# RG-LRU coefficients from an exponential of the gate, and a 16-token decay product moved to GpSimd, in a two-layer hybrid trunk

## The chip, the cores and the metric

The kernel runs on one core of a Trainium2 chip. The metric is the device time of one execution, in microseconds (us); the time of a kernel is the median of its runs. The engines are named as in the profile: PE is TensorE (matmuls; PEld is its weight load), DVE is VectorE, ACT is ScalarE, POOL is GpSimd, and SP issues the DMAs. A row's line number is a line of the kernel before.

## The reference, cut to what matters

Two layers, each a feed-forward half step, a mixing step with four mixers side by side (A: RG-LRU, B: gated delta rule, C: SSD, D: S5), and a second feed-forward half step, on 272 tokens of width 1024. The change touches mixer A and one product of mixer C:

```python
def rglru_mixer(u_x, u_gate, conv_w, conv_b, w_a, b_a, w_i, b_i, lam, norm_g):
    xc = (causal_dwconv(u_x, conv_w) + conv_b).astype(F32)
    ...
    r = jax.nn.sigmoid(... xh, w_a ... + b_a)
    ig = jax.nn.sigmoid(... xh, w_i ... + b_i)
    log_a = -LRU_C * r * jax.nn.softplus(-lam.astype(F32))     # LRU_C = 8
    a = jnp.exp(log_a)
    b = jnp.sqrt(-jnp.expm1(2.0 * log_a)) * (ig * xc)
    _, h = lax.associative_scan(_linear_combine, (a, b), axis=1)
    y = jax.nn.gelu(u_gate.astype(F32)) * h
    return rms_norm(y, norm_g)
...
    # mixer C, in ssd_chunked: scores of a chunk times their decays
    y_diag = jnp.einsum("bcgls,bcgels,bcsgep->bclgep", cb, lmat, x)
```

## The kernel before, in words

Activations lie feature-major: 128 features on the partitions, 272 tokens (256 in the last layer, after the mixing) on the free axis. All projection weights come from HBM in chunks of 128x1024 (512 KB), three raw buffers deep (`load`). For each chunk `ahead` makes two pieces, `hi` by a copy on ACT (L215) and `lo` by a subtraction on DVE (L217), four buffers deep, and PE multiplies a chunk in 24 matmuls of three kinds (`mm3`, L232 to L234). These chunk matmuls, called g matmuls below after their PSUM tile `g`, are the bulk of PE's time; those of the mixers themselves write PSUM tiles `m`, of which there are four.

The mixing step is a list of steps written out by hand (`STEPS_TEXT`). The list gives each instruction its priority; the scheduler of the tile framework (`schedule_with_timeline_sim=True`) makes from it one fixed order for each engine, putting a step of later priority ahead where its model of the time has an engine free and the earlier step not ready. On the chip each engine goes through its own order strictly, so an instruction that waits holds up all that are behind it on its engine.

In the list the steps that matter here come as `... am2 am1 ... am0 ... am3 bs04 bf12 S0 bf13 ce0 bf14 ag0 bs10 bs11 cz3 bs12 ac ag1 bs13 bs14 bz0 S1 bz1 as0 ...`:

- `am0` to `am3` (`a_gates`): for each of the four 128-feature blocks, two matmuls, three tanh on ACT (L887, L888, L889) and a product on DVE (L890). L888 makes t = tanh(-log_a/2) into the tile `s5a` (`at_`).
- `ac` (`a_coef`): from t it makes a = 2/(1+t) - 1 and sqrt(1-a^2) = 2 sqrt(t)/(1+t). Four square roots on ACT (L897) after a load of ACT's function table; for each block a sum (L901), a reciprocal (L902) and a multiply-add (L903) on DVE and two products on POOL (L904, L905), the last into `s5b` (`ab_`).
- `as0` to `as3` (`a_scan`): the recurrence, on DVE (L915).
- `bs00` to `bs14` (`b_solve`) and `bf00` to `bf14` (`b_factor`): the triangular solve of mixer B, a serial chain between PE (L686) and ACT or DVE. `bf14` copies a factor `f4t` from PSUM on ACT (L707, tile `rk`); `bs10` subtracts the first block's part on DVE (L722, tile `rs`). The PE step `bs11` (L686, `m<-rs,rk`) needs both of them.
- `S0`, `S1` (`decay_in`): 10 small copies on ACT each (L501), the input of the decay matmuls of `ce0` and `ce1`.
- `ce0` to `ce3` (`c_decay`): decay matmuls (L517 to L525), three exponentials on ACT (L528), then the product with the scores: 832 columns on POOL (L815) and the last 16 tokens on DVE (L816). `cp0` to `cp3` (`c_pair`) multiply the result on PE (L826).

Temporary tiles `r` are a ring of nine, given out in the order of the list.

Of the kernel before, what the change touches and what calls it, by code (L numbers as in the profile page):

```python
# [12 lines left out]
AF = mybir.ActivationFunctionType  # L13
ALU = mybir.AluOpType
AX = mybir.AxisListType.X

P = 128
T = 272
# [99 lines left out]
class Trunk:  # L118
# [693 lines left out]
    def c_decay(s, i):  # L812
        e = s.ce[i] = s.decay(s.R[2 + i])
        gt = s.cg[:, i // 2:i // 2 + 1, :]
        s.nc.gpsimd.tensor_tensor(out=e[:, :, 0:416], in0=gt[:, :, 0:416].to_broadcast([P, 2, 416]), in1=e[:, :, 0:416], op=ALU.mult)  # L815
        s.nc.vector.tensor_tensor(out=e[0:16, :, 416:432], in0=gt[0:16, :, 416:432].to_broadcast([16, 2, 16]), in1=e[0:16, :, 416:432], op=ALU.mult)  # L816


    def c_pair(s, i, l):
# [24 lines left out]
    def a_consts(s):  # L844
        nc = s.nc
        c = COLS
        cut = lambda n: s.sm[:, :, c[n][0]:c[n][0] + c[n][1]]

        m = s.tiny([P, 2, 4], 'lm')
        nc.vector.tensor_scalar(out=m, in0=cut('llam'), scalar1=-1.0, scalar2=None, op0=ALU.mult)  # L850
        sp = s.softplus(m, [P, 2, 4])
        s.sp2 = s.const([P, 2, 4], 'sp2')
        nc.vector.tensor_scalar(out=s.sp2, in0=sp, scalar1=2.0, scalar2=None, op0=ALU.mult)
        s.hb = s.const([P, 2, 8], 'hb')
        o = c['lba'][0]
        nc.vector.tensor_scalar(out=s.hb, in0=s.sm[:, :, o:o + 8], scalar1=0.5, scalar2=None, op0=ALU.mult)
# [21 lines left out]
    def a_gates(s, i, l):  # L878
        nc = s.nc
        xc, w = s.ab_[:, i, :], s.lw[i]  # L880
        pr, pi = s.mps(), s.mps()
        nc.tensor.matmul(pr[:, 0:T], lhsT=w[:, 0, :], rhs=xc, start=True, stop=True)
        nc.tensor.matmul(pi[:, 0:T], lhsT=w[:, 1, :], rhs=xc, start=True, stop=True)
        t = s.at_[:, i, :]
        sp = s.sp2[:, l, i:i + 1]
        r, g = s.tmp(), s.tmp()
        nc.scalar.activation(out=r, in_=pr[:, 0:T], func=AF.Tanh, scale=0.5, bias=s.hb[:, l, i:i + 1])  # L887
        nc.scalar.activation(out=t, in_=r, func=AF.Tanh, scale=sp, bias=sp)  # L888
        nc.scalar.activation(out=g, in_=pi[:, 0:T], func=AF.Tanh, scale=0.5, bias=s.hb[:, l, 4 + i:5 + i])  # L889
        nc.vector.scalar_tensor_tensor(out=xc, in0=g, scalar=1.0, in1=xc, op0=ALU.add, op1=ALU.mult)  # L890


    def a_coef(s):
        nc = s.nc
        sq = [s.tmp() for _ in range(4)]
        for i in range(4):
            nc.scalar.activation(out=sq[i], in_=s.at_[:, i, :], func=AF.Sqrt)  # L897
        for i in range(4):
            t, b = s.at_[:, i, :], s.ab_[:, i, :]
            r = s.tmp()  # L900
            nc.vector.tensor_scalar(out=t, in0=t, scalar1=1.0, scalar2=None, op0=ALU.add)  # L901
            nc.vector.reciprocal(out=r, in_=t)  # L902
            nc.vector.tensor_scalar(out=t, in0=r, scalar1=2.0, scalar2=-1.0, op0=ALU.mult, op1=ALU.add)  # L903
            nc.gpsimd.tensor_tensor(out=b, in0=b, in1=sq[i], op=ALU.mult)  # L904
            nc.gpsimd.tensor_tensor(out=b, in0=b, in1=r, op=ALU.mult)  # L905

    def a_gate(s, ps, i):
        if i == 0:
# [404 lines left out]
    def mixing(s, l, sl, done):  # L1313
        s.R, s.be, s.ce, s.bm, s.bo, s.cacc = ({} for _ in range(6))
        s5 = {}
        s.sl, s.N = sl, sl.stop - sl.start

        def small():
            s.sm16 = s.tokens(s.small_tile())

        def d_in(u):
            s5[u] = s.d_load(l, u)
            s.d_in(u, s5[u])

        def rin(i):
            s.R[i] = s.decay_in(i)

        def chain():
            with s.tc.issue_after(s.last_dve):
                s.b_chain()  # L1330

        do = dict(
            sm=small, tk=lambda: s.token_scalars(s.sm16, l), R=rin, S=lambda i: rin(2 + i),
            di=d_in, do=lambda u: s.d_out(u, s5[u]), da=lambda f: s.d_act(f, l), ds=s.d_split, dg=s.d_glu, dn=lambda j: s.d_norm(l, j),
            ks=lambda i: s.b_sums('k', i), qs=lambda i: s.b_sums('q', i), bn=lambda: s.b_norms(), bv=s.b_values, be=s.b_decay, bg=s.b_gram,
            bb=lambda: s.b_blocks(), bc=chain, bm=s.b_masks, bf=s.b_factor, bs=s.b_solve, bt=s.b_tail, bo=lambda h, j: s.b_out(h, l, j),
            xd=s.c_xdt, cg=s.c_gram, ce=s.c_decay, cp=lambda i: s.c_pair(i, l), cn=lambda g, j: s.c_norm(g, l, j),
            am=lambda i: s.a_gates(i, l), ac=lambda: s.a_coef(), an=lambda j: s.a_norm(l, j))
        do['as'] = s.a_scan
        full = slice(0, T)  # L1340
        pss = s.first_tiles(full)
        s.norm_x(s.col('nm', l), full)
        s.ahead(AHEAD)
        n, outs = 0, [0, 0]
        for name, a in STEPS:
            if name in IN:
                s.unit(name, a[0], pss[n] if n < NF else s.one_tile(sl if name in ('ag', 'bz', 'cz') else full), l)
                n += 1
            elif name in OUT:
                q = a[0]  # L1350
                s.out_tiles(q, OUT[name], outs[q] == 0, outs[q] == 3, sl, done)
                outs[q] += 1
            else:
                do[name](*a)
# [160 lines left out]
```

## Time and profile before

| | |
|---|---|
| median of 3 runs | 1447.62 us (1442.08, 1447.62, 1450.54) |
| the profiled execution | 1442.42 us, of which the span from first to last instruction is 1440.5 us |
| busy share of the span | PE 97%, PEld 94%, DVE 72%, ACT 49%, POOL 14% |
| mean granted TensorE clock | 0.969 of 2.4 GHz |
| moved | 222.16 MB read, 19.78 MB written |

The first mixing step lies at about 225 to 510 us of the span, the second at about 950 to 1215 us; the rest is feed-forward. A busy share is an average over stages with different limits, and matmuls are pipelined with modelled ends, so a busy PE is not PE at its peak: a stretch at half the granted clock is busy too. In the rows, a time in brackets is idle time ahead of an instruction with what ended it, and the shapes are partitions x elements.

### The profile page before, as it was taken

To read this page: it belongs to the slowest core of one execution; us is meant where nothing else is said; L and a number is where in the kernel's file an instruction comes from. 1 tells how busy PE (TensorE), PEld (TensorE's weight loads), DVE (VectorE), ACT (ScalarE), POOL (GpSimd) and SP (SyncE) were. 2 spreads that over 40 slices of the span, in tenths; PEclk is the share of its full clock that TensorE was granted. 3 is DMA by queue.
4 is the path that set the end of the run, shared out by engine and by line. 5 is a ranking of instruction groups with operands and counts; after the bars stand their busy time and mean duration, and the time that the engine had idled before them with its cause. 6 is when DMAs were issued, how large, how long until landed. Compare 5 with 4: busy or idle time off the path is not lost. (4 is left out here: it accounts for less than half of the span.)

```text
span 1440.5 us, 27604 instructions
## 1 busy us (share of the span) xinstructions
PE 1392.0 (97%) x10848; PEld 1353.8 (94%) x10848; DVE 1036.4 (72%) x1936; ACT 708.4 (49%) x1226; POOL 205.4 (14%) x235
## 2 busy tenths in 40 slices
PE   7999999998999999999999999999989899999997
PEld 7999998997998999999999999989989889999997
DVE  6998787978985468887656665669888746666653
ACT  6445444454675355554444444444555745544442
POOL 1000010322322320000100000103332223100011
PEclk9999999999997999999999999999999979999998
DMA  7568775654422256777555555556544213666662
GB/s 238 179 188 265 235 254 163 217 171 120 126 77 71 82 155 217 254 230 254 172 162 184 175 170 174 172 161 211 177 127 141 74 45 114 186 187 187 188 182 85
DMA packets 94025, 243.73 MB, mean 169 GB/s; under 512 B 29496, under 2 KB 39496, under 8 KB 93896
## 3 DMA queue, kind: packets, MB, share of 16 engines
q1 hardware_dynamic: 93896, 241.97, 54.2%
q8 instruction: 85, 1.39, 0.4%
q14 instruction: 44, 0.36, 0.1%
HBM read 222.16 MB, written 19.78 MB: 168 GB/s over the span
## 5 line engine op out<-in xcount | busy, mean ns | idle before, releaser
L215 ACT ACTIVATE hi<-raw 128x1024 fp32r<-128x1024 f32 (+1 forms) x382 | 403.3, 1056 | 532.2 <-PE g L233 302.0
L217 DVE TENSOR_TENSOR lo<-raw,hi 128x1024 fp32r<-128x1024 f32 (+1 forms) x382 | 470.2, 1231 | 215.6 <-ACT hi L215 213.9
L232 PE MATMUL g<-xh,hi 128*128 128x272 f32 (+1 forms) x2048 | 597.7, 293 | 12.2 <-ACT hi L215 8.7
L234 PE MATMUL g<-xh,lo 128*128 128x272 f32 (+1 forms) x2048 | 595.8, 292 | 0.8 <-DVE lo L217 0.8
L233 PE MATMUL g<-xl,hi 128*128 128x272 f32 (+1 forms) x2048 | 595.3, 291 | 0.3 <-DVE xl L317 0.3
L232 PEld LDWEIGHTS g<-xh,hi 128*128 128x128 f32 x2048 | 391.4, 191 | 14.7 <-ACT hi L215 8.6
L234 PEld LDWEIGHTS g<-xh,lo 128*128 128x128 f32 x2048 | 390.7, 191 | 2.6 <-DVE lo L217 1.1
L233 PEld LDWEIGHTS g<-xl,hi 128*128 128x128 f32 x2048 | 391.5, 191 | 1.5 <-DVE xl L317 0.6
L277 POOL TENSOR_TENSOR acc<-acc,r 128x272 f32<-128x272 f32 (+1 forms) x42 | 43.3, 1032 | 556.1 <-ACT r L276 555.4
L233 PE MATMUL g<-r,hi 128*128 128x272 f32 (+1 forms) x256 | 73.2, 286 | 0.0
L360 DVE TENSOR_TENSOR r<-r,g 128x272 f32<-128x272 f32 (+1 forms) x88 | 38.1, 432 | 37.5 <-PE g L234 36.0
L545 DVE SCALAR_TENSOR_TENSOR r<-g,small,r 128x269 f32<-128x269 f32 (+2 forms) x120 | 59.1, 493 | 2.0 <-ACT r L542 0.4
L234 PE MATMUL g<-ra,lo 128*128 128x272 f32 (+1 forms) x192 | 55.2, 287 | 0.0
L232 PE MATMUL g<-ra,hi 128*128 128x272 f32 (+1 forms) x192 | 55.1, 287 | 0.0
L233 PE MATMUL g<-rs,hi 128*128 128x272 f32 (+1 forms) x192 | 55.0, 286 | 0.0
L233 PE MATMUL g<-rz,hi 128*128 128x272 f32 (+1 forms) x192 | 55.0, 286 | 0.0
L234 PE MATMUL g<-rq,lo 128*128 128x272 f32 (+1 forms) x192 | 54.6, 287 | 0.0
L232 PE MATMUL g<-rq,hi 128*128 128x272 f32 (+1 forms) x192 | 53.5, 289 | 0.2
L358 DVE TENSOR_TENSOR r<-g,rstd 128x272 f32<-128x272 f32 (+1 forms) x88 | 38.3, 435 | 15.6 <-PE g L234 14.8
L233 PEld LDWEIGHTS g<-r,hi 128*128 128x128 f32 x256 | 48.1, 188 | 0.0
L232 PE MATMUL g<-dU,hi 128*128 128x272 f32 (+1 forms) x96 | 29.7, 309 | 9.8 <-DVE r L545 9.8
L359 ACT ACTIVATE r<-r 128x272 f32<-128x272 f32 (+1 forms) x88 | 36.5, 415 | 5.4 <-DVE r L358 4.2
(412 smaller groups left out, 2461.5 us busy)
## 6 DMA issues: line engine op xcount, KB each, us to landing
raw<-in_wgu_dram SPq DMA_DIRECT2D x176, 512.0 KB
raw<-in_wdn_dram SPq DMA_DIRECT2D x88, 512.0 KB
raw<-in_win_dram SPq DMA_DIRECT2D x80, 512.0 KB
raw<-in_wout_dram SPq DMA_DIRECT2D x32, 512.0 KB
s5a<-spill SPq DMA_DIRECT2D x8, 920.0 KB
s5b<-spill SPq DMA_DIRECT2D x8, 896.0 KB
spill<-s5a SPq DMA_DIRECT2D x8, 648.0 KB
spill<-rx SPq DMA_DIRECT2D x4, 640.0 KB
```

Source lines behind the costliest of these rows:

```text
L215: nc.scalar.activation(out=hi[:, 0:w], in_=raw[:, 0:w], func=AF.Copy)
L217: ins = nc.vector.tensor_tensor(out=lo[:, 0:w], in0=raw[:, 0:w], in1=hi[:, 0:w].bitcast(F32), op=ALU.subtract)
L232: nc.tensor.matmul(ps, lhsT=hi, rhs=xh, start=start, stop=False)
L233: nc.tensor.matmul(ps, lhsT=hi, rhs=xl, start=False, stop=False)
L234: nc.tensor.matmul(ps, lhsT=lo, rhs=xh, start=False, stop=stop)
L277: (eng or nc.gpsimd).tensor_tensor(out=acc, in0=acc, in1=t, op=ALU.add)
L358: nc.vector.tensor_tensor(out=t, in0=g[:, t0], in1=r, op=ALU.mult)
L359: nc.scalar.activation(out=si, in_=t, func=AF.Silu)
L360: nc.vector.tensor_tensor(out=a, in0=si, in1=u[:, t0], op=ALU.mult)
L545: nc.vector.scalar_tensor_tensor(out=dst[:, o:T], in0=ps[:, 0:T - o], scalar=taps[:, j:j + 1], in1=dst[:, o:T], op0=ALU.mult, op1=ALU.add)
```

## The change

`ac` no longer divides. `am` stops at the first tanh th of the recurrence gate, which goes straight into `at_`. `ac` makes t = tanh(sp2(1+th)) into a temporary and a = exp(-4 softplus (1+th)) in place, both on ACT, then sqrt(t/4) on ACT; DVE forms (a+1)*b in one instruction for each block, and POOL multiplies by the root once. So 1/(1+t) is read as (1+a)/2. A small constant `sp4` is made once. The 16-token product of `ce` goes from DVE to POOL, behind the large one.

```diff
     def c_decay(s, i):
...
         s.nc.gpsimd.tensor_tensor(out=e[:, :, 0:416], in0=gt[:, :, 0:416].to_broadcast([P, 2, 416]), in1=e[:, :, 0:416], op=ALU.mult)
-        s.nc.vector.tensor_tensor(out=e[0:16, :, 416:432], in0=gt[0:16, :, 416:432].to_broadcast([16, 2, 16]), in1=e[0:16, :, 416:432], op=ALU.mult)
+        s.nc.gpsimd.tensor_tensor(out=e[0:16, :, 416:432], in0=gt[0:16, :, 416:432].to_broadcast([16, 2, 16]), in1=e[0:16, :, 416:432], op=ALU.mult)
...
     def a_consts(s):
...
+        s.sp4 = s.const([P, 2, 4], 'sp4')
+        nc.vector.tensor_scalar(out=s.sp4, in0=sp, scalar1=-4.0, scalar2=None, op0=ALU.mult)
...
     def a_gates(s, i, l):
...
-        t = s.at_[:, i, :]
-        sp = s.sp2[:, l, i:i + 1]
-        r, g = s.tmp(), s.tmp()
-        nc.scalar.activation(out=r, in_=pr[:, 0:T], func=AF.Tanh, scale=0.5, bias=s.hb[:, l, i:i + 1])
-        nc.scalar.activation(out=t, in_=r, func=AF.Tanh, scale=sp, bias=sp)
+        g = s.tmp()
+        nc.scalar.activation(out=s.at_[:, i, :], in_=pr[:, 0:T], func=AF.Tanh, scale=0.5, bias=s.hb[:, l, i:i + 1])
...
-    def a_coef(s):
+    def a_coef(s, l):
         nc = s.nc
         sq = [s.tmp() for _ in range(4)]
         for i in range(4):
-            nc.scalar.activation(out=sq[i], in_=s.at_[:, i, :], func=AF.Sqrt)
+            t, p2, p4 = s.at_[:, i, :], s.sp2[:, l, i:i + 1], s.sp4[:, l, i:i + 1]
+            nc.scalar.activation(out=sq[i], in_=t, func=AF.Tanh, scale=p2, bias=p2)
+            nc.scalar.activation(out=t, in_=t, func=AF.Exp, scale=p4, bias=p4)
         for i in range(4):
-            t, b = s.at_[:, i, :], s.ab_[:, i, :]
-            r = s.tmp()
-            nc.vector.tensor_scalar(out=t, in0=t, scalar1=1.0, scalar2=None, op0=ALU.add)
-            nc.vector.reciprocal(out=r, in_=t)
-            nc.vector.tensor_scalar(out=t, in0=r, scalar1=2.0, scalar2=-1.0, op0=ALU.mult, op1=ALU.add)
+            nc.scalar.activation(out=sq[i], in_=sq[i], func=AF.Sqrt, scale=0.25)
+        for i in range(4):
+            b = s.ab_[:, i, :]
+            nc.vector.scalar_tensor_tensor(out=b, in0=s.at_[:, i, :], scalar=1.0, in1=b, op0=ALU.add, op1=ALU.mult)
             nc.gpsimd.tensor_tensor(out=b, in0=b, in1=sq[i], op=ALU.mult)
-            nc.gpsimd.tensor_tensor(out=b, in0=b, in1=r, op=ALU.mult)
```

## Rows read from the trace of the kernel before

**Rows 1.** Waits of PE: engine, line, releaser; total us, times, longest us.

```profile
PE m L686 <- DVE E L816: 4.9, 1, 4.9
```

**Rows 2.** Windows around the two waits: us, busy times (instructions), granted clock, DMA share, GB/s.

```profile
412.00:427.00 15.00, 14.94 (x117) 14.34 (x115) 14.98 (x15) 14.51 (x37) 8.19 (x9) 1.00 0.20 66
427.00:449.00 22.00, 20.52 (x161) 18.36 (x161) 19.31 (x36) 9.90 (x20) 3.77 (x3) 1.00 0.48 144
...
1126.00:1138.30 12.30, 12.29 (x101) 11.70 (x99) 11.02 (x14) 12.26 (x28) 6.12 (x8) 1.00 0.08 33
1138.30:1143.20 4.90, 0.00 (x0) 0.01 (x1) 4.90 (x8) 4.37 (x13) 3.21 (x2) 0.93 0.64 170
...
1142.60:1149.40 6.80, 6.14 (x27) 5.88 (x28) 4.94 (x11) 0.91 (x3) 0.00 (x0) 0.50 0.44 138
```

**Rows 3.** Timeline of PE at both waits: start us, us, instruction, [idle before].

```profile
422.60 1.06 PE L686 MATMUL m<-rz,rn 128*128 128x128 f32 x8
428.24 1.13 PE L686 MATMUL m<-rs,rk 128*128 128x128 f32 x8 [1.29 <-DVE rs L722]
...
1136.88 1.05 PE L686 MATMUL m<-rz,rn 128*128 128x128 f32 x8
1143.22 2.05 PE L686 MATMUL m<-rs,rk 128*128 128x128 f32 x8 [4.93 <-DVE E L816]
```

**Rows 4.** Timeline of DVE, second layer, ahead of PE's wait's end.

```profile
1142.40 0.68 DVE L722 TENSOR_TENSOR rs<-rs,m 128x512 f32<-128x512 f32 x1
1142.99 0.17 DVE L816 TENSOR_TENSOR E<-rg,E 16x32 f32<-16x32 f32 x1
```

**Rows 5.** Groups by line, 409.9 to 427.5 us: count, busy us, mean ns, idle before.

```profile
L902 DVE RECIPROCAL r<-s5a 128x272 f32<-128x272 f32 x4 | 7.1, 1812 | 0.0
L901 DVE TENSOR_SCALAR s5a<-s5a 128x272 f32<-128x272 f32 x4 | 2.7, 707 | 0.4 <-ACT r L897 0.4
L903 DVE TENSOR_SCALAR s5a<-r 128x272 f32<-128x272 f32 x4 | 2.5, 653 | 0.0
```

**Rows 6.** Timeline of DVE and ACT, a gate step of the first layer: prices.

```profile
401.98 0.43 DVE L890 SCALAR_TENSOR_TENSOR s5b<-r,s5b 128x272 f32<-128x272 f32 x1
...
400.42 0.61 ACT L888 ACTIVATE s5a<-r,sp 128x272 f32<-128x272 f32 x1
400.94 0.47 ACT L889 ACTIVATE r<-m,hb 128x272 f32<-128x272 f32 x1
```

**Rows 7.** Timeline of ACT, second layer, the stretch in which it is full.

```profile
1125.92 1.28 ACT L897 ACT_TABLE_LOAD   x1
1127.21 1.39 ACT L897 ACTIVATE r<-s5a 128x272 f32<-128x272 f32 x4
...
1136.16 0.92 ACT L501 ACTIVATE r<-cst,ghr 128x272 fp32r<-128x272 f32 x2
...
1140.04 0.58 ACT L707 ACTIVATE rk<-m 128x512 f32<-128x512 f32 x1
```

**Rows 8.** Timeline of ACT, first layer: exponential, copy, then a tanh.

```profile
423.40 0.43 ACT L528 ACTIVATE E<-m 128x320 f32<-128x320 f32 x1
...
424.12 0.59 ACT L707 ACTIVATE rk<-m 128x512 f32<-128x512 f32 x1
424.59 0.43 ACT L864 ACTIVATE r<-r 128x272 f32<-128x272 f32 x1
```

**Rows 9.** A shorter idle of PE, second layer: window, then the timeline after it.

```profile
1070.60:1074.30 3.70, 3.67 (x17) 3.53 (x18) 2.61 (x8) 2.00 (x5) 0.00 (x0) 0.54 0.11 41
...
1070.63 0.36 PE L232 MATMUL g<-dU,hi 128*128 128x256 f32 x1 [3.87 <-DVE r L545]
```

**Rows 10.** Timeline of POOL and of PE at the last decay product.

```profile
1135.77 0.78 POOL L905 TENSOR_TENSOR s5b<-s5b,r 128x272 f32<-128x272 f32 x1 [2.06 <-DVE r L902]
1197.79 1.97 POOL L815 TENSOR_TENSOR E<-rg,E 128x832 f32<-128x832 f32 x1 [1.78 <-ACT E L528]
...
1200.06 0.44 PE L826 MATMUL m<-E,rx 128*64 128x256 f32 x2
```

## What the change should do to the time

> **What bounds the kernel now.** I read the page's busy shares first: PE is busy for 97% of the span, so only the time in which PE waits, or works at the lower clock, can be won back. Next I read the waits of PE over the whole span. Where the change works, the longest is that of PE's solve step L686, 4.9 us in one piece [rows 1]. The timeline of PE places it at 1143.22 us, in the second layer, ahead of the step `bs11` (`m<-rs,rk`), and shows a smaller one of 1.29 us ahead of the same step of the first layer, at 428.24 us [rows 3]. The larger wait is put down to L816, but that is only the DVE instruction that ended last: L722, which makes `rs`, starts at 1142.40 and takes 0.68 us, so it ends at 1143.08, and PE starts 0.14 us later [rows 3, 4]. In the first layer the wait is put down to L722 itself [rows 3]. So both waits are for L722.
>
> L722 could have run much earlier. Its input is PE's product `m<-rz,rn`, which ends at 423.66 in the first layer and at 1137.93 in the second [rows 3]. `bs11` starts 4.6 and 5.3 us after that, of which 0.14 + 0.68 + 0.14 = 1.0 us are L722 and the two hand-overs. The other 3.6 and 4.3 us L722 stands in DVE's queue, which is full: 14.98 of 15 us before the first wait, and all of the 4.90 us of the second [rows 2]. In that queue stand the sums, reciprocals and multiply-adds of `ac`.
>
> The windows show what the waits cost. In the first layer the clock stays at 1.00 (2.4 GHz) after the wait. In the second, PE goes on at 0.50 (1.2 GHz) from 1142.6 to 1149.4 us, 6.8 us [rows 2]. The 6.14 us of work in it would take half at the full clock, so 3.1 us are lost there. All that can be won directly is thus 1.3 + 4.9 + 3.1 = 9.3 us.
>
> The same windows warn of the other engine. ACT is busy 14.51 of 15 us and 12.26 of 12.30 us in the stretches ahead of the waits [rows 2], and the change puts work exactly there.
>
> **The change part by part.** *Off DVE.* Four reciprocals, four sums and four multiply-adds go: 7.1 + 2.7 + 2.5 = 12.3 us in the first layer [rows 5]. Four fused products come, each priced by L890, the same operation and shape, at 0.43 us [rows 6]: 1.7 us. DVE's queue ahead of L722 gets 10.6 us shorter, far more than the 3.6 and 4.3 us by which L722 is late. So L722 would run as soon as its input is there: done 0.14 + 0.68 us after 1137.93, at 1138.75 us.
>
> *Onto ACT.* The second tanh (L888) of each block moves from the gates into `ac`, and four exponentials are new. L888 has the same form as both (128x272, scale and bias by column): 0.61 us alone, and its successor starts 0.52 us after it [rows 6]. Eight of them are 4.2 us, put in ahead of the roots, in the full stretch. What is taken out of the gates, half of that, frees ACT some 10 us earlier, where no wait of PE is named; I count it as nothing. Tanh follows an exponential without a table load [rows 8], so tanh and exponential change nothing there: the loads stay one before the roots, 1.28 us [rows 7], and one of its kind before the next exponential.
>
> *What is late next.* When L722 is early, `bs11` waits for its other input, L707 on ACT. In the first layer L707 ends at 424.71 [rows 8], and PE wants it at 426.95 (the start of its wait), so ACT may be 2.2 us later at no cost. In the second layer L707 ends at 1140.62 [rows 7] and PE wants it at 1138.29, so even with an unchanged ACT only about 4.93 - 2.46 = 2.5 us (PE's start at 1140.76 in place of 1143.22) can be won there.
>
> Where the added 4.2 us land in ACT's order the trace of before can't show, so I bound it. If all of it goes ahead of L707, L707 ends at 1144.82 and PE starts at 1144.96, 1.7 us later than now; in the first layer L707 ends at 428.91 and PE starts 0.8 us later than now. If none goes ahead of it, 2.5 and 1.3 us are won. Between these lies the case that the scheduler keeps the priorities: `bf14` (L707) is ahead of `ac` and `S1` in the list, and the copies of `S1` that ran ahead of L707 give way. They fill the time from 1136.16 to L707's start at 1140.04, 3.9 us, but for two exponentials of `ce0` at 0.43 us at most [rows 7, 8], so they are 3.0 us. Then L707 is 4.2 - 3.0 = 1.2 us later. I take this value, since a fuller ACT in the scheduler's model is what lets L707 pass: PE starts at about 1142.0, and 1.2 us are won; in the first layer 1.2 us are inside the 2.2 us of cover, and all of 1.3 us is won.
>
> *The clock.* The second layer's idle time becomes 1142.0 - 1138.3 = 3.7 us. The nearest row is an idle time of 3.87 us: after it PE ran at about half the clock for one window of 3.7 us (0.54) [rows 9], while after 4.93 us it did for 6.8 us [rows 2]. So I count half of the present loss as won back: 1.6 us. The bounds are 0 and 3.1 us.
>
> *POOL.* Four products (L905), 0.78 us each, go in each layer. They and L904 feed the scans, which nobody waits for by the waits read. Four 16x32 products come. Two sizes of the same operation, 272 columns in 0.78 us and 832 in 1.97 us [rows 10], give 2.1 ns a column and 0.2 us fixed, so 0.27 us for 32 columns; the bounds are L816's own 0.17 us [rows 4] and the 0.78 us. Behind it on POOL stand the norm powers (L254) and the next large product, and PE's L826 waits for it. The tightest place is the last one of the second layer: L815 ends at 1199.76 and L826 starts at 1200.06 [rows 10], 0.30 us of cover against 0.27. I cost it at 0, bounds 0 to 0.5 us a layer. The Trainium skill's page "GPSIMD Engine Reference", section "Engine selection", advises against such a move: an elementwise product of two inputs is about twice as slow there. By that factor the product would take 0.34 us and the sum would grow by less than 0.1 us; no run here shows it yet.
>
> The constant `sp4` is one DVE instruction of 8 columns in the first feed-forward step, where PE never waits: 0. The weight loads go past nothing new on SP; DVE frees raw buffers earlier, which can only bring them forward.
>
> *Sum.* First layer 1.3, second layer 1.2 + 1.6, POOL 0: 4.1 us. Against the profiled execution, 1442.42 us (span 1440.5), that gives 1438.3. The median of the runs, 1447.62, lies 5.2 us above that execution; the gain is taken off the median: 1443.5 us.
>
> **The rivals.** *The whole of the waits goes.* If the scheduler also lets PE do chunk matmuls while L707 comes, or puts L707 before the added work, then `bs11` costs nothing and the clock stays up: 9.3 us, 1438.3 us. For it: the list is re-ordered around a DVE queue that is 10.6 us shorter, and PE has g matmuls in every part of the mixing step that can stand in a gap. Against it: L707 at 1140.62 is late by itself.
>
> *ACT takes DVE's place.* The added 4.2 us go ahead of L707 in both layers: 0.8 + 1.7 us later than now, 2.5 us slower, 1450.1 us. For it: ACT is as full as DVE was. Against it: `ac` stands behind `bf14` in the list.
>
> *Slower: the roots are torn apart by the exponentials of `ce0`.* The roots now come 4.2 us later, about when the decay matmuls of `ce0` are done, and `ce0` is ahead of `ac` in the list. If one of its exponentials falls between two roots, two more table loads are needed, 2 x 1.28 = 2.6 us, and L707 is up to 6.8 us later: 3.4 us beyond now in the first layer, 4.3 in the second. The first layer's idle time is then 4.7 us, about that of the second layer now, and costs 3.1 us of clock as well: 10.8 us in all, 1458.4 us. It decides from the point at which a root stands behind an exponential in ACT's order, that is from more than two loads a layer on. The Trainium skill's page "ScalarE: Activation LUTs", section "What ACT_TABLE_LOAD costs", gives about 2.66 us for each change of table with its drain. By it, two more changes would be 5.3 us a layer and this rival 16.2 us, 1463.8 us. The trace shows the load at 1.28 us and the next root 0.01 us behind it, so the row's price is the one that I use.
>
> **How the numbers follow.** Forecast, 1443.5 us: 0.37. The whole of the waits: 0.34. ACT in DVE's place: 0.15. Torn roots: 0.14. About 0.5% (7.2 us) is what a measurement of this kernel can tell from no change. The forecast and the second rival are inside it, the first rival is faster by more, the torn roots are slower by more: faster 0.34, same 0.52, slower 0.14. The range goes from the first rival's time less 5.5 us, the distance of the lowest run of before below its median (1432.8, rounded to 1433), to the second rival's plus 2.9, that of the highest above it (1453). It leaves out the torn roots.
>
> **What would show it.** Right: no reciprocal on DVE, L722 within 1 us of its input, PE's wait ahead of `bs11` gone in the first layer and 2 to 3.5 us in the second, now ended by ACT's L707, two table loads a layer, and a stretch at 0.50 near 1142 of at most about 3.5 us. Wrong: a wait of PE ended by an L501, L729 or L707 that is longer than now (ACT is the bound), more than two table loads a layer, L826 waiting on POOL by more than 0.5 us, or a changed order that moves the two long stretches of small matmuls at the end of each mixing step, for which this sum has no term.

## The result, and the profile after

The changed kernel is slower: median 1451.16 us of 20 runs (1444.03 to 1460.64) against 1443.77 us of 20 runs of before (1438.73 to 1450.54), ratio 1.0052, 95% interval 1.0034 to 1.0070, so 7.5 us. Its profiled execution took 1453.98 us (span 1452.3) beside 1442.42 us (span 1440.5) of before.

By the two pages VectorE is busy for 1017.3 us, 19 us less than in before, ACT for 713.3 us, 5 us more, and PE for 1395.4 us, 3.4 us longer. ACT has ten instructions more (1236 for 1226): the eight exponentials, and two table loads that the change does not intend.

To find where the 11.8 us between the spans lie, I cut both at the same instructions: the first matmul of the recurrence's gates (`m<-s5b`) and an addition to the residual (L1309: the fourth of the first mixing step, the last of the second); the two mixing steps' stretches are shown. Windows of before, then of after; columns: us, busy time and instructions of PE, its weight loads, DVE, ACT, POOL, then granted clock, DMA share, GB/s.

```profile
396.17:508.29 112.12, 109.90 (x765) 100.24 (x764) 71.47 (x129) 63.42 (x141) 31.88 (x35) 0.91 0.26 79
...
1112.52:1241.84 129.32, 122.74 (x896) 114.46 (x895) 80.28 (x135) 71.95 (x152) 31.78 (x29) 0.89 0.32 95
```

```profile
401.36:513.37 112.01, 109.72 (x765) 100.03 (x764) 61.77 (x117) 64.99 (x145) 30.14 (x35) 0.91 0.26 79
...
1119.22:1253.94 134.72, 123.30 (x896) 113.93 (x895) 71.92 (x123) 75.93 (x158) 25.12 (x29) 0.90 0.30 91
```

The first stretch begins 5.2 us later (401.36 for 396.17), although ahead of it PE's order is the same. At 250.95 us PE met a wait of 2.37 us for a DMA (`dU<-ud`, 0.4 us in before) and ran at half the clock behind it. That wait belongs to the execution: act_work below, which lacks the change, shows it too (1.8 us), and roots_last, which has the change, shows none of 1 us or more. The late start is not explained by it, though: roots_last begins 4.1 us late as well (400.25). Of the 15 profiled executions the ten with the change begin this stretch at 397.2 to 404.1 us, the five without it at 396.2 to 398.0, with granted clocks from 225 us to there of 0.91 to 0.95 and of 0.93 to 0.94. In after only the one instruction for `sp4` is new ahead of it (VectorE, 226.51 us, so not in the feed-forward step as I had it); whether it has a part in this no run tests.

The first layer's stretch is as long as before (112.01 for 112.12), the second's is 5.4 us longer, 4.8 of them idle time of PE (length less busy time: 11.42 for 6.58); what lies between the two grew by 1.6 us. So in these two executions the change gained nothing in the first layer and lost in the second. Two single waits of PE are placed below; a third kind, for L726, comes three times behind them in the second layer (5.8 us in all, the longest 3.0; in before 0.4 us in all).

*First layer.* The timelines of DVE, ACT and PE at `bs11`, for [rows 3] and [rows 8]:

```profile
431.65 0.69 DVE L722 TENSOR_TENSOR rs<-rs,m 128x512 f32<-128x512 f32 x1 [0.63 <-PE m L686]
...
432.86 0.58 ACT L707 ACTIVATE rk<-m 128x512 f32<-128x512 f32 x1
...
433.49 1.16 PE L686 MATMUL m<-rs,rk 128*128 128x128 f32 x8 [1.38 <-ACT rk L707]
```

L722 now waits for PE's product and is no longer late. But PE waits 1.38 us where it waited 1.29, now for ACT's L707. ACT has taken VectorE's place.

*Second layer.* The timeline of ACT, for [rows 7], then DVE and PE behind it:

```profile
1134.55 0.60 ACT L899 ACTIVATE s5a<-s5a,sp 128x272 f32<-128x272 f32 x1
1135.17 1.28 ACT L901 ACT_TABLE_LOAD   x1
1136.46 0.43 ACT L901 ACTIVATE r<-r 128x272 f32<-128x272 f32 x1
...
1140.72 1.28 ACT L899 ACT_TABLE_LOAD   x1
1142.01 1.62 ACT L899 ACTIVATE s5a<-s5a,sp 128x272 f32<-128x272 f32 x3
1143.65 1.28 ACT L901 ACT_TABLE_LOAD   x1
1144.95 1.07 ACT L901 ACTIVATE r<-r 128x272 f32<-128x272 f32 x3
1146.04 1.28 ACT L866 ACT_TABLE_LOAD   x1
1147.33 0.42 ACT L866 ACTIVATE r<-r 128x256 f32<-128x256 f32 x1
...
1147.78 0.42 DVE L867 SCALAR_TENSOR_TENSOR dp<-r,g 128x256 f32<-128x256 f32 x1 [3.67 <-ACT r L866]
...
1148.25 0.58 PE L232 MATMUL g<-xh,hi 128*128 128x256 f32 x1 [4.43 <-DVE dp L867]
...
1159.28 1.05 PE L686 MATMUL m<-rs,rk 128*128 128x128 f32 x8
```

One exponential of `ac` (L899) and one root (L901) ran early, then the other three exponentials, then the other three roots: four table loads where before had two. The tanh of the gate's gelu (L866) stands behind the last of them, and PE needs the PSUM bank that the gelu still reads: 4.43 us of waiting. VectorE itself was idle for 3.67 us there. The wait of 4.93 us at `bs11` [rows 3] is gone (last row); this one, and those for L726, stand in its place.

### The profile page after: what moved, and what is told of

It is laid out like the page before. It is cut to its first block, busy times and chain, and to the rows that moved or that the text cites. A ratio compares the mean times of both kernels' runs of the same rounds, so it can differ in the third digit from the quotient of the medians.

```text
span 1452.3 us, 27577 instructions
## 1 busy us (share of the span) xinstructions
PE 1395.4 (96%) x10848; PEld 1355.3 (93%) x10848; DVE 1017.3 (70%) x1913; ACT 713.3 (49%) x1236; POOL 197.6 (14%) x235
## 3 DMA queue, kind: packets, MB, share of 16 engines
q8 instruction: 86, 1.41, 0.4%
## 5 line engine op out<-in xcount | busy, mean ns | idle before, releaser
L217 DVE TENSOR_TENSOR lo<-raw,hi 128x1024 fp32r<-128x1024 f32 (+1 forms) x382 | 468.6, 1227 | 215.1 <-ACT hi L215 213.7
```

Source lines behind the costliest of these rows:

```text
L217: ins = nc.vector.tensor_tensor(out=lo[:, 0:w], in0=raw[:, 0:w], in1=hi[:, 0:w].bitcast(F32), op=ALU.subtract)
```

## The experiments

Ratios are against the kernel before, run on the same chip beside it, with 95% intervals; the times are medians of 12 runs (after 20, s1_behind 6). Each edit also lets the scheduler make a new order for every engine; where the text names the order as unchanged or changed, that is read from the traces.

| kernel | what it is | median us | ratio |
|---|---|---|---|
| after | the change | 1451.16 | 1.0052 [1.0034, 1.0070] |
| roots_last | after, the four roots behind the last exponential | 1446.22 | 1.0009 [0.9988, 1.0030] |
| torn_l2 | roots_last, torn in layer 2 | 1452.33 | 1.0044 [1.0019, 1.0068] |
| torn_l1 | roots_last, torn in layer 1 | 1447.54 | 1.0016 [0.9998, 1.0035] |
| no_recip | before, no reciprocals | 1440.09 | 0.9972 [0.9955, 0.9990] |
| act_work | before, 8 more ACT instructions a layer | 1445.60 | 1.0004 [0.9976, 1.0032] |
| in_gates | after, tanh and exponential in `am` | 1439.23 | 0.9964 [0.9939, 0.9989] |
| in_gates_dve | in_gates, small product on VectorE | 1438.81 | 0.9953 [0.9934, 0.9973] |
| gates_torn | in_gates_dve, torn in layer 2 | 1443.07 | 1.0001 [0.9983, 1.0018] |
| pool_only | before, small product on GpSimd | 1446.60 | 1.0009 [0.9987, 1.0030] |
| s1_behind | roots_last, decay copies behind L707 | 1454.80 | 1.0073 [1.0047, 1.0098] |
| gates_s1 | in_gates_dve, decay copies behind L707 | 1443.40 | 0.9988 [0.9964, 1.0011] |
| big_dve | before, large decay product on VectorE | 1447.49 | 1.0017 [0.9990, 1.0044] |
| gates_big_dve | in_gates_dve, the same | 1438.33 | 0.9959 [0.9939, 0.9979] |

### The tear: roots_last, torn_l2, torn_l1, gates_torn

roots_last against after:

```diff
-            nc.scalar.activation(out=t, in_=t, func=AF.Exp, scale=p4, bias=p4)
-        for i in range(4):
-            nc.scalar.activation(out=sq[i], in_=sq[i], func=AF.Sqrt, scale=0.25)
+            last = nc.scalar.activation(out=t, in_=t, func=AF.Exp, scale=p4, bias=p4)
+        with s.tc.issue_after(last.ins):
+            for i in range(4):
+                nc.scalar.activation(out=sq[i], in_=sq[i], func=AF.Sqrt, scale=0.25)
```

> The changed kernel with one thing undone: the four roots are issued only behind the last of the four exponentials of `ac`, so no root of the second layer can stand between two exponentials. Nothing else changes. Theory T (the tear): the second layer's two additional table loads and the late tanh of the gelu behind them are what cost the about 7 us between the last matmuls of the two profiles. Then: two loads a layer around the roots in place of four in layer 2, the wait of PE for the gelu's PSUM bank (4.43 us, put down to DVE's `dp`) gone or under 1.5 us, and the median 1442 to 1446 us where the kernel before has 1443.8, ratio 0.998 to 1.002. Theory A (ACT's added work): the exponentials and tanh themselves, 8 x 0.52 us in a full stretch of ACT, are what costs, whatever their order. Then the loads are two a layer all the same, but PE's waits in the second layer stay within a third of what they are in the changed kernel, and the median stays at 1449 to 1452 us, ratio over 1.003.

Timeline of ACT and PE, second layer:

```profile
1137.87 1.65 ACT L899 ACTIVATE s5a<-s5a,sp 128x272 f32<-128x272 f32 x3
1139.53 1.28 ACT L902 ACT_TABLE_LOAD   x1
1140.82 1.39 ACT L902 ACTIVATE r<-r 128x272 f32<-128x272 f32 x4
1142.23 1.28 ACT L866 ACT_TABLE_LOAD   x1
1143.53 0.42 ACT L866 ACTIVATE r<-r 128x256 f32<-128x256 f32 x1
...
1144.45 0.39 PE L232 MATMUL g<-xh,hi 128*128 128x256 f32 x1 [1.59 <-DVE dp L867]
```

The tear is gone, PE's wait is 1.59 us in place of 4.43, and 0.43% of the time with it: 6.2 us, give or take 4 (the two half-widths added as squares, 0.18% and 0.21%). But the kernel is level with before, not faster. Theory T holds for the loss, with one reserve: PE's order differs between the two in 27 places, so this pair prices the tear together with the order that it brought. The gain is still missing.

torn_l2 puts one column's exponential between the first root and the other three, in layer 2 alone:

```diff
         with s.tc.issue_after(last.ins):
-            for i in range(4):
+            last = nc.scalar.activation(out=sq[0], in_=sq[0], func=AF.Sqrt, scale=0.25)
+        if l == 1:
+            with s.tc.issue_after(last.ins):
+                last = nc.scalar.activation(out=s.tear, in_=s.hb[:, l, 0:1], func=AF.Exp)
+        with s.tc.issue_after(last.ins):
+            for i in range(1, 4):
                 nc.scalar.activation(out=sq[i], in_=sq[i], func=AF.Sqrt, scale=0.25)
```

> The kernel with the roots last, and one exponential of a single column set between the first root of the second layer and its other three. It adds two table loads (2 x 1.28 us) and one instruction of some 0.2 us to ACT, and nothing else of the order around it changes. Theory L (the two loads by themselves are the cost of the tear): the tanh of the gelu comes 2.8 us later, the wait of PE for the gelu's PSUM bank grows from 1.59 to 4.4 us, and the median goes up by 5 to 9 us against the kernel with the roots last, to a ratio of 1.0035 to 1.007 against before, that of the changed kernel. Rival O (the order is the cost: in the changed kernel the first root ran ahead of the copies and of L707, and three exponentials behind them): the loads alone cost their own length at most, up to 2.8 us, ratio under 1.003.

```profile
1149.82 0.43 ACT L902 ACTIVATE r<-r 128x272 f32<-128x272 f32 x1
1150.26 1.28 ACT L905 ACT_TABLE_LOAD   x1
1151.56 0.20 ACT L905 ACTIVATE tear<-hb 128x1 f32<-128x1 f32 x1
1151.77 1.28 ACT L908 ACT_TABLE_LOAD   x1
...
1155.44 0.42 ACT L867 ACTIVATE r<-r 128x256 f32<-128x256 f32 x1
...
1156.37 0.58 PE L232 MATMUL g<-xh,hi 128*128 128x256 f32 x1 [4.49 <-DVE dp L868]
```

From the first root to the gelu's tanh it is 5.62 us here and 2.71 with the roots last: 2.91 us more, and PE's wait is 2.90 us longer. The time is that of after again (1.0044 and 1.0052). The order is that of roots_last but for three instructions each of PE, VectorE and ACT that stand elsewhere in the second layer, so the loads themselves make that wait longer, one for one. Against roots_last the time is 0.35% more, half-width 0.32%: by the time alone rival O (2.8 us at most) is not excluded.

> The same in the first layer alone: two table loads more between its first root and its other three, the second layer as in the kernel with the roots last. There L707 is what PE waits for ahead of `bs11` (1.38 us with the roots last). If ACT is the bound there, L707 comes 2.8 us later and the wait grows to 4.2 us; with half the clock behind it (as behind the 4.93 us of before, [rows 2]) the cost is 2.8 + up to 3.1 us, so 3 to 6 us against the kernel with the roots last, ratio 1.003 to 1.005 against before. Rival: PE fills the time with chunk matmuls that stand later in its order, the wait grows by less than 1.5 us, ratio under 1.0025.

torn_l1 is the same with `l == 0`. PE's waits in the first layer:

```profile
428.44 1.16 PE L686 MATMUL m<-rz,rn 128*128 128x128 f32 x8 [1.71 <-ACT E L528]
431.99 2.07 PE L686 MATMUL m<-rs,rk 128*128 128x128 f32 x8 [2.01 <-ACT rk L707]
```

3.7 us of waits where the roots-last kernel has 1.38: PE did wait some 2.3 us longer, but the medians differ by 0.07%, half-width 0.28%: anything from 3 us faster to 5 us slower. Neither theory is excluded.

gates_torn has the same tear in in_gates_dve (below), which has tanh and exponential out of `ac`:

> The kernel with tanh and exponential in `am` and the small product on VectorE (0.9953, interval 0.9934 to 0.9973), with one exponential of a single column set between the first root of the second layer and its other three: two table loads and some 0.3 us more on ACT, 2.9 us as measured in the torn kernel with the roots last, nothing else of the order changed. Theory F (the loads cost because ACT is full there and the gelu's tanh stands behind them): here the tanh behind the roots runs 8 to 9 us before PE's solve step and PE does not wait for it; L707 is 2.9 us later, at PE's solve step at most some tenths, ratio 0.9935 to 0.9980, no PE wait of over 1 us put down to `dp` or L707. Theory W (two loads cost PE their length wherever they stand): a wait of some 2.9 us that the kernel without them does not have, and 3 to 5 us, ratio 0.9975 to 0.9990.

It lost 0.48% (1.0001 for 0.9953; 6.9 us, give or take 3.8), outside what theory F allows. That does not show that loads cost where ACT has room, because ACT has none here either: it is busy 20.30 of the 20.40 us from the first load on (1129.10 to 1149.50). Theory W's wait of 2.9 us is not there. The longest new wait is half of it, for a copy that stands behind the loads on ACT, and the second stretch is only 1.5 us longer than in in_gates_dve (127.64 for 126.16):

```profile
1137.87 0.50 PE L517 MATMUL m<-r,ugt 128*128 128x256 f32 x2 [1.41 <-ACT r L501]
```

Three pairs (after and roots_last, torn_l2 and roots_last, gates_torn and in_gates_dve) thus price two more loads in the second layer at 0.43%, 0.35% and 0.48%, 5 to 7 us. The last two, which keep the order almost as it was, give 0.42% as their mean, half-width 0.21%: 3.0 to 9.0 us, just clear of the 2.9 us that the loads add to ACT.

### What the relief of VectorE is worth: no_recip and act_work

no_recip drops three lines of `ac` from before; the second GpSimd product takes the tanh itself.

```diff
-            r = s.tmp()
-            nc.vector.tensor_scalar(out=t, in0=t, scalar1=1.0, scalar2=None, op0=ALU.add)
-            nc.vector.reciprocal(out=r, in_=t)
-            nc.vector.tensor_scalar(out=t, in0=r, scalar1=2.0, scalar2=-1.0, op0=ALU.mult, op1=ALU.add)
-            nc.gpsimd.tensor_tensor(out=b, in0=b, in1=r, op=ALU.mult)
+            nc.gpsimd.tensor_tensor(out=b, in0=b, in1=t, op=ALU.mult)
```

> The kernel before without the sums, reciprocals and multiply-adds of `ac` on VectorE (L901 to L903 left out, and the second GpSimd product takes the tanh itself, so the recurrence's coefficients are not the reference's). ACT does exactly what it does before; it measures what the relief of VectorE is worth alone. By the prediction's steps: L722 comes within 1 us of its input, PE's wait ahead of `bs11` goes in the first layer (1.3 us), in the second 2.5 us of 4.9 are won until L707 ends at 1140.62, and 1.6 to 3.1 us of clock: 5.4 to 6.9 us, ratio 0.9953 to 0.9963, 1437 to 1438.5 us. Rival: the wait only changes its owner (PE waits for L707, or the late DVE work behind it) and the median stays within 2 us of before (ratio over 0.9985).

Timeline of PE, both layers:

```profile
427.37 1.05 PE L686 MATMUL m<-rs,rk 128*128 128x128 f32 x8
...
1140.81 1.05 PE L686 MATMUL m<-rs,rk 128*128 128x128 f32 x8
1147.95 1.16 PE L686 MATMUL m<-rs,rv 128*128 128x128 f32 x8 [1.44 <-DVE rs L726]
1151.16 2.08 PE L686 MATMUL m<-rs,rk 128*128 128x128 f32 x8 [2.05 <-DVE rs L726]
```

Both waits ahead of `bs11` are gone, and 4.0 us (1.4 to 6.5) are won; two waits for L726, 3.5 us together, open behind them. The prediction's reading of the bound holds, and its 5.4 to 6.9 us lie at its upper end and beyond. The path is another one: by the prediction PE would still wait for L707 in the second layer, with 2.5 of the 4.9 us to be won. Here the whole wait goes, since PE does g matmuls until `bs11`, and the loss comes later, at L726.

act_work was to add the ACT work alone to the same stretch of before:

```diff
+        d = s.a3[:, 0:T]
+        for i in range(4):
+            nc.scalar.activation(out=d, in_=s.at_[:, i, :], func=AF.Tanh)
+            last = nc.scalar.activation(out=d, in_=s.at_[:, i, :], func=AF.Exp)
+        with s.tc.issue_after(last.ins):
             for i in range(4):
                 nc.scalar.activation(out=sq[i], in_=s.at_[:, i, :], func=AF.Sqrt)
```

> The kernel before with four tanh and four exponentials of 128x272 more a layer on ACT, into memory that nobody reads, ahead of the four roots; the reciprocals stay on VectorE, and nothing else changes. It is ACT's addition to that stretch (4.2 us a layer by the prediction's price) without VectorE's relief. By the prediction's rival of ACT in place of VectorE: L707 up to 4.2 us later, 0.8 us in the first layer and 1.7 us in the second, and no more, since VectorE holds PE back anyway: +2.5 us, ratio 1.0017. If a full ACT costs PE more than L707 alone (late copies, gelu and PSUM banks, half clock): +4 to +8 us, ratio 1.003 to 1.0055. If ACT's idle time ahead of the stretch takes it in: ratio 0.9985 to 1.0010.

Timeline of ACT, then of PE:

```profile
404.69 0.41 ACT L898 ACTIVATE a<-s5a 128x272 f32<-128x272 f32 x1
...
429.94 1.24 PE L686 MATMUL m<-rs,rk 128*128 128x128 f32 x8 [2.47 <-DVE E L816]
...
1155.24 2.04 PE L686 MATMUL m<-rs,rk 128*128 128x128 f32 x8 [5.26 <-DVE E L816]
```

The work did not land in the full stretch. Each of the eight needs only the `at_` of its own block, and the scheduler set them among the gates' steps, where ACT had room: 404.69 to 411.16 us in the first layer, all ahead of the table load at 411.78, which comes only 0.9 us later behind the gates' first matmul than in before (14.74 for 13.81 us). The waits grow by 1.2 and 0.3 us, still behind VectorE, and the time does not move within 0.3%: the third case expected. So this run says nothing on the rival of ACT in VectorE's place; roots_last and in_gates have to tell.

### The same work at another place: in_gates, in_gates_dve

```diff
 (a_gates)
+        nc.scalar.activation(out=s.t4[i], in_=t, func=AF.Tanh, scale=p2, bias=p2)
         nc.scalar.activation(out=g, in_=pi[:, 0:T], func=AF.Tanh, scale=0.5, bias=s.hb[:, l, 4 + i:5 + i])
+        nc.scalar.activation(out=t, in_=t, func=AF.Exp, scale=p4, bias=p4)
 (a_coef)
-            nc.scalar.activation(out=sq[i], in_=t, func=AF.Tanh, scale=p2, bias=p2)
-            nc.scalar.activation(out=t, in_=t, func=AF.Exp, scale=p4, bias=p4)
...
-            nc.scalar.activation(out=sq[i], in_=sq[i], func=AF.Sqrt, scale=0.25)
+            nc.scalar.activation(out=sq[i], in_=s.t4[i], func=AF.Sqrt, scale=0.25)
```

> The changed kernel with the same work at another place: the second tanh and the new exponential of each block run in `am`, right behind the gate's first tanh, and only the four roots are left in `ac` (the second tanh goes to memory of its own that is free at that time). ACT does just as much as in the changed kernel, but not in the full stretch. By theory T (the tear): no exponential of `ac` can stand between the roots, two loads a layer, so 1442 to 1446 us like the kernel with the roots last. By theory A (ACT's added work in the full stretch): the 4.2 us are out of that stretch and VectorE is relieved by 10.6 us a layer, so this is the first form that brings the gain, 1436 to 1441 us (ratio 0.995 to 0.998), with PE's waits ahead of `bs11` at most 0.5 us in the first layer and 2.5 us in the second. Both can hold; then the roots-last kernel gives the share of the first and this one the rest. Against both: four tanh and exponentials earlier push other ACT work of the gates' stretch, which would show as PE waits for L886 or L887.

```profile
432.26 1.05 PE L686 MATMUL m<-rs,rk 128*128 128x128 f32 x8
...
1144.45 1.05 PE L686 MATMUL m<-rs,rk 128*128 128x128 f32 x8
```

No wait ahead of `bs11` in either layer, two loads a layer, two waits for L726 behind it as without the reciprocals (1.46 and 2.05 us), and 0.45% less time than with the same instructions inside `ac` (roots_last; half-width 0.33%). So the arithmetic of the change does bring its gain, 5 us (1.6 to 8.8). In after ACT is busy 7.15 of the 13.70 us of the gates' steps and 18.38 of the 18.44 us from the second tanh to PE's `bs11` (first layer): put into `ac`, the work meets the full stretch, and the gain is not seen.

> The kernel with tanh and exponential in `am`, and the product of the last 16 tokens back on VectorE: what is left is the exponential in place of the reciprocals alone. If the move of the product to GpSimd is worth nothing, as the kernel with that move alone says within 0.2%, the ratio against before is that of the kernel with both (0.9964, interval 0.9939 to 0.9989), so 0.994 to 0.9985. If the freed VectorE makes the 8 x 0.17 us worth something once the reciprocals are gone, it is 0.5 to 2 us slower than that. If GpSimd was a cost hidden until now, it is faster, under 0.9955.

With the small product back on VectorE the ratio is 0.9953: the two are not told apart (0.11%, half-width 0.32%). This kernel, with gates_big_dve beside it at 0.9959, is the fastest form found, ahead of both kernels.

### The small product: pool_only

> The kernel before with one part of the change alone: the product of the last 16 tokens goes from VectorE to GpSimd. Theory of the prediction: 4 products a layer at 0.24 us (the changed kernel's rows for L816), no wait of PE for it, so the time is that of before within 1 us (ratio 0.9995 to 1.0005, resolved to some 0.2%). Rival: VectorE and GpSimd meet in the scans' tail, the large product L815 or L905 on GpSimd waits behind it and PE's last gathers are later: 2 to 4 us slower (ratio 1.0015 to 1.003), with a wait of L826 for GpSimd of over 0.5 us.

1.0009, so nothing that can be measured (up to 0.3%). In after seven of the eight products take 0.24 us and the last one 0.43; PE waits for none.

### Do the copies have to give way? s1_behind, gates_s1

```diff
-            nc.scalar.activation(out=flat, in_=ps, func=AF.Copy)
+            s.last_f = nc.scalar.activation(out=flat, in_=ps, func=AF.Copy)
...
+        def later(i):
+            with s.tc.issue_after(s.last_f.ins):
+                rin(2 + i)
-            ... S=lambda i: rin(2 + i),
+            ... S=later,
```

> The kernel with the roots last, and the copies of the decay inputs (L501) of each step issued behind the solve's copy that the list has ahead of them (`S0` behind L707 of `bf12`, `S1` behind that of `bf14`). It is the step of the prediction that the scheduler did not take: that the copies give way to L707. Between the roots and L707 `rk` the kernel with the roots last has copies of 3.4 us in the first layer and 3.0 us in the second. Theory P (the copies are what keeps L707 late, and L707 is what VectorE's relief is lost to): L707 comes some 3 us earlier against the roots, PE's wait of 1.38 us ahead of `bs11` goes in the first layer, and the time comes down by 3 to 6 us, to a ratio of 0.996 to 0.999 against before. Rival Q (L707 is only one of several late things on a full ACT; what is put behind it is late in its turn): the ratio stays where the roots-last kernel is, 1.000 to 1.003.

It has the highest ratio of all, 1.0073 (0.64% above roots_last, half-width 0.33%, from six runs). L707 came 1.3 us earlier in the first layer, not 3 (429.32 us, with the gates' first matmul at 399.16; 431.75 and 400.25 with the roots last), yet PE waited longer. Timelines of ACT, POOL, DVE and PE:

```profile
429.32 0.62 ACT L707 ACTIVATE rk<-m 128x512 f32<-128x512 f32 x1
...
429.52 2.00 POOL L815 TENSOR_TENSOR E<-rg,E 128x832 f32<-128x832 f32 x1 [1.47 <-ACT E L528]
...
429.81 2.01 DVE L918 TENSOR_TENSOR dp<-dp,r 128x272 f32<-128x272 f32 x1
431.74 0.67 DVE L722 TENSOR_TENSOR rs<-rs,m 128x512 f32<-128x512 f32 x1
...
432.56 1.75 PE L686 MATMUL m<-rs,rk 128*128 128x128 f32 x8 [2.54 <-ACT r L501]
```

The wait is put down to a copy that ended with it, but L722 ended at 432.41, 0.15 us ahead of PE: it stood behind L918, which took 2.01 us where others of its kind take 0.4, while GpSimd multiplied (below). That is rival Q's kind of cause, though the time lies above its 1.000 to 1.003, and PE's order differs from that of roots_last in 60 places.

> The same order of the copies in the kernel with tanh and exponential in `am` and the product of the last 16 tokens on VectorE (0.9953, interval 0.9934 to 0.9973). There PE has no wait ahead of `bs11` any more in either layer, so by theory P the copies are worth nothing there: 0.993 to 0.9975. By rival Q something else on ACT moves with them: over 0.9985 where the copies come late for `ce0`, `as` and what follows.

There, too, the copies behind L707 cost: 0.9988 for 0.9953, 0.35%, half-width 0.30%. Theory P falls in s1_behind; here the cost is only just clear of the noise.

### A product of GpSimd that holds VectorE: big_dve, gates_big_dve

In before, two timelines side by side in the first layer, POOL and DVE:

```profile
423.91 1.98 POOL L815 TENSOR_TENSOR E<-rg,E 128x832 f32<-128x832 f32 x1 [1.02 <-ACT E L528]
...
424.24 1.81 DVE L903 TENSOR_SCALAR s5a<-r 128x272 f32<-128x272 f32 x1
```

The two runs move that product (L815) to VectorE.

> The kernel before with the large decay product (L815, 128x832) on VectorE in place of GpSimd; nothing else changes. In the trace of before VectorE's L903 takes 1.81 us at 424.24 and 2.25 us for two at 1140.23, both times while L815 runs on GpSimd (423.91 to 425.89 and 1139.82 to 1142.11); alone, one takes 0.29 us (427.11). Both stand ahead of L722, for which PE waits. Theory H (VectorE is held while GpSimd multiplies two tiles, and that was a part of the waits ahead of `bs11`): L903 takes 0.3 to 0.4 us everywhere, L722 comes 0.5 to 1.7 us earlier (the product itself is 1.0 us on VectorE by L217's 1.21 us for 1024 columns, ahead of L722 or behind it), PE's waits of 1.29 and 4.93 us shrink by as much, ratio 0.997 to 1.000. Rival N (the slow L903 has another cause): one or more L903 of over 1 us stay, and VectorE has 1.0 us more ahead of L722: the waits grow, ratio 1.000 to 1.002.

Groups by line, first layer, for [rows 5]; then the timeline of PE:

```profile
L903 DVE TENSOR_SCALAR s5a<-r 128x272 f32<-128x272 f32 x4 | 1.0, 274 | 0.0
L815 DVE TENSOR_TENSOR E<-rg,E 128x832 f32<-128x832 f32 x1 | 1.0, 1012 | 0.0
```

```profile
427.84 1.13 PE L686 MATMUL m<-rs,rk 128*128 128x128 f32 x8 [0.72 <-DVE rs L722]
...
1144.69 1.13 PE L686 MATMUL m<-rs,rk 128*128 128x128 f32 x8 [3.18 <-DVE rs L722]
1147.71 0.58 PE L232 MATMUL g<-xh,hi 128*128 128x256 f32 x1 [1.89 <-DVE dp L865]
```

The four L903 take 1.0 us in place of 2.5, and the waits ahead of `bs11` shrink from 1.29 to 0.72 and from 4.93 to 3.18 us: theory H, shown for the hold. The sums ahead (L901, 2.7 us [rows 5]) are slow in the same way beside another product of GpSimd (L904, 411.79 to 415.07): one alone takes 0.23 us (1132.71). No run moves that one. No time is won (1.0017, interval 0.9990 to 1.0044): 1.0 us of product a step came to VectorE, and a wait of 1.89 us opened behind it.

> The same move in the kernel with tanh and exponential in `am` and the small product on VectorE (0.9953, interval 0.9934 to 0.9973), the fastest so far. Theory H: VectorE has room there since the reciprocals are gone, and is no longer held at L815; PE's waits for L726 behind `bs11` (1.45 and 2.05 us) shrink where a product of GpSimd holds what is ahead of them, ratio 0.993 to 0.997. Rival N: four products of 1.0 us a layer more on VectorE, which then comes late for L726 and the scans: ratio 0.996 to 1.000.

0.9959 beside 0.9953: no difference there either.

## Why the prediction was right or wrong

The time lay in the range, but the sign was wrong: I forecast 4.1 us less, the kernel took 7.5 us more. I gave 0.34 to faster, 0.52 to the same and 0.14 to slower. That the time lay in the range was luck: I took the gain off 1447.62, the median of three runs, and 20 runs give 1443.77. From there the same steps give 1439.7 us and a range of 1429 to 1449, which the measured 1451.16 is outside of. The step that failed is the term for ACT's table loads, which I put at nothing beyond what is there; the copies' place and the clock's 1.6 us failed beside it.

- *The bound: right.* PE waits for L722 in VectorE's queue; without the reciprocals both waits vanish (no_recip). Two parts of the queue were misread: 1.5 of the 2.5 us of the multiply-adds [rows 5], and by the same sign most of the sums' 2.7 us, were VectorE held by GpSimd's products, not work.
- *ACT's price: right.* Eight instructions at 0.52 us were 4.2 us; with the roots last they take 2.12 + 0.61 + 1.65 = 4.4 us in the second layer.
- *Table loads: the step that failed first.* I counted two a layer. The first layer has two, the second four, which was one of my signs of being wrong; undoing it takes off 6.2 us, give or take 4 (roots_last). I had the torn roots as a rival, with two loads, 2.6 us, as price (2.9 us measured, with the torn-in instruction), but at a chance of 0.14 and with the wrong culprit: not the exponentials of `ce0` but the exponentials of `ac` itself, which I had put ahead of the roots as a block. Nothing in the program holds them there: a root depends only on its own block's tanh. The rival's path was wrong too: PE met the delay through the gelu's tanh and a PSUM bank (4.43 us), not through L707 at `bs11`.
- *The copies give way: wrong.* I took L707 as 1.2 us later in the first layer. It is 3.5 us later (432.86 against 424.12, less the 5.2 us by which this execution was late before), as copies of 3.4 us still stood ahead of it: only two (0.5 us) had moved behind it. From the cover of 2.2 us it follows that PE waits 1.3 us; it waited 1.38. The arithmetic was right and the choice between the bounds wrong, and forcing the choice did not help (s1_behind).
- *The gain: it exists but not there.* Of the 4.1 us of the sum, nothing came in the first layer, and the roots-last kernel, the change without its tear, is level with before. The rival of ACT in VectorE's place, at 0.15, is what the first layer shows. In the second, roots_last has no wait at `bs11` at all; 1.59 us for the gelu and 4.4 us for L726 stand behind it, and my sum had no term for either. Its profiled second stretch is still 3.6 us shorter than before's (125.69 for 129.32, at a clock of 0.95 for 0.89), its first as long (112.02), and it began 4.1 us late: where the gain went the medians don't say.
- *GpSimd: right.* 0.24 us measured (the last one 0.43), 0.27 estimated, no wait of L826, no change of time.
- *The clock: nothing won.* I counted 1.6 us. In the second layer's stretch the granted clock is 0.90 (0.89 before), and PE is busy 0.6 us longer, not shorter (123.30 for 122.74): the wait of 4.43 us has a stretch at 0.51 behind it, as that of 4.93 us had.

What stays open: two loads cost 2.9 us of ACT, and 5 to 7 us by the medians of three pairs. In torn_l2 a wait of just 2.9 us is seen, in gates_torn of 1.4 us. A part of the rest can be the clock right behind the longer wait. Windows of after (behind its 4.43 us) and of roots_last (behind its 1.59 us):

```profile
1148.20:1151.60 3.40, 3.35 (x15) 3.35 (x16) 2.93 (x4) 3.40 (x7) 0.00 (x0) 0.51 0.16 19
```

```profile
1144.40:1148.60 4.20, 4.15 (x35) 4.15 (x36) 3.49 (x5) 4.20 (x10) 0.28 (x1) 1.00 0.24 66
```

torn_l2 has 5.04 us of work at 0.50 behind its 4.49 us, and gates_torn 3.30 us at 0.50 behind its 1.41 us, where in_gates_dve runs at 1.00. At half of that work each, an estimate from these rows, it is 1.7, 2.5 and 1.7 us beside longer waits of 2.8, 2.9 and 1.4: 4.5, 5.4 and 3.1 us. That is not proof. torn_l1 has such a stretch too (5.71 us of work at 0.50 behind its 2.01 us), and its median hardly moves. Over the whole second stretch in_gates_dve and gates_torn have the same clock (0.91): the stretches at half clock come and go between executions. torn_l1 and roots_last issue the second layer in almost the same order, and the same stretch of it (as cut above) differs by 4.5 us with the granted clock; first roots_last, then torn_l1:

```profile
1118.24:1243.93 125.69, 117.14 (x896) 108.52 (x895) 71.74 (x122) 72.93 (x156) 28.18 (x29) 0.95 0.32 98
```

```profile
1116.79:1247.01 130.22, 120.87 (x896) 111.60 (x895) 71.73 (x122) 73.13 (x156) 28.14 (x29) 0.91 0.31 95
```

## What to carry to other kernels

When a change adds a function from another table set to a block of instructions that a scheduler orders, tie the block together (here: all roots behind the last exponential), or it can be torn at each ready instruction and pay for two loads. Where work moves from a full engine to one that is just as full in that stretch, the wait changes its owner and nothing is won; move it to where the second engine has idle time, here in the gates' steps ahead of it, and the gain can appear (0.9964 here). Look at the instructions ahead of a late one for durations far over their kind's: they can be held by another engine (here GpSimd), and no price by kind shows it. Taking the hold away need not win time (1.0017 here).

## What the runs showed of the hardware

A table load is 1.28 us and the next instruction starts 0.01 us behind it; two of them with a 0.20 us instruction moved the next tanh by 2.91 us. The Trainium skill's page "ScalarE: Activation LUTs", section "What ACT_TABLE_LOAD costs", gives about 2.66 us for each change, by which an estimate for two is 5.3 us; the rows here are half of that, though the time of the whole kernel went up by 5 to 7 us.

GpSimd and VectorE hold each other up: L903 alone takes 0.29 us, and 1.81 us while GpSimd's product runs, ending 0.16 us after it; GpSimd's L905 takes 0.78 us [rows 10], and 1.55 us at 1137.67, beside VectorE's L217 of 1137.45 to 1138.60. The Trainium skill's page "SBUF — State Buffer", section "Who interferes with whom", says that the two share one pair of ports under an exclusive lock; these rows, and big_dve, agree. The product took 2.0 us on GpSimd and 1.01 us on VectorE, about the factor of two that the prediction cites; the 16x32 one took 0.24 for 0.17, less than that factor.
